# A hybrid decoder block on one core: one copy out of a product's bank queued later, one block's gate values in another buffer, and the first chunk of terms loaded from ScalarE's queue

## The chip, the cores and the metric

The kernel runs on one core of one Trainium2 chip. The metric is the device time of one execution in microseconds (us), as the median of several runs. The core has five engines that each run their own queue of instructions in order and wait for each other through semaphores: TensorE (PE in the profile; it multiplies matrices, its weight loads are listed apart as PEld), VectorE (DVE), ScalarE (ACT), GpSimd (POOL) and SyncE (SP), which here only issues transfers. Transfers (DMA) are issued by SyncE, ScalarE or GpSimd and carried out by 16 DMA engines. TensorE writes its results into banks of PSUM; everything else lies in SBUF.

## The reference

The input is 512 tokens of width 2048 in float32. One RMS norm feeds one input projection, whose columns go to two attention mixers (a dilated sliding window one with 8 heads and a sparse one with compressed, selected and window branches, 8 heads). Their normed outputs go through one output projection and are added to the input. Then comes the part that matters here, a gated feed-forward layer with 5632 hidden columns, and a final norm:

```
hn2 = rmsnorm(h, norm2_g[l])
h = h + (jax.nn.silu(hn2 @ w_gate[l]) * (hn2 @ w_up[l])) @ w_down[l]
return rmsnorm(h, final_g)
```

## The kernel before

**Precision.** A float32 matrix product is made of three products of a faster type. Each operand is split into a high part (a rounded copy, made by ScalarE, L176) and a low part (operand minus high part, made by VectorE, L179), and high by high, high by low and low by high are added in PSUM (L1018 to L1020). A block of weights is 128 x 1024 and arrives by a transfer into a buffer named raw; its two parts go into a buffer named w, of which there are three, so the split for a product can start when the product three places before it has ended.

**Seven products.** The feed-forward layer is computed in blocks of 128 hidden columns, 44 of them (f = 0 to 43). The weights of one block form a 2 x 2 scheme, gate and up by the two halves of the model width; the activations form another, the halves of the width by the two halves of the tokens (LO and HI, 256 tokens each). A scheme of Strassen's kind replaces the eight products of such a 2 x 2 multiplication by seven, P1 to P7, of 24 matmuls each. They run in the order P1, P5, P6, P2, P7, P3, P4 (block 0 in another one). The right operands are seven fixed "terms" of the activations, B11, T1, T2, B21, T3, B22, T4 in that same order, each in a high and a low part; T2, T3 and B22 lie in the tiles named ah and al. The left operands are combinations of the four weight quadrants A11, A12, A21, A22. Y is A21 + A22, made by a load from SyncE and a second load that GpSimd issues and that adds on top (L138); X is A21, or A21 + A11 made in the same way. VectorE makes the further combinations in place (L807).

**Banks.** P1, P6, P7 and P4 accumulate into one bank of PSUM, E; P5 and P3 into F; P2 has G. Between them the bank's value so far has to be taken out: after P1 by g1 (ScalarE, L1128, into the left half of the gate tile g), after P5 by g5 (ScalarE, L1132, into the right half of the tile u), after P6 by g6 (L1135). So P6 may not start before g1 has read E, and P3 not before g5 has read F. VectorE adds the later banks on top, the Silu is taken (L1147), and u becomes the hidden block. g and u are taken from a ring of two buffers with the tag "ft". In block 0 the same is done by gate0: a Silu on ScalarE (L1186) and a multiplication on VectorE (L1187) end it, and these two run while block 1 has begun. A second ring of two buffers, tag "r", serves for factors that are spread over the partitions.

**Down projection.** Pairs of hidden blocks are turned into the seven terms of the next multiplication and stored to DRAM by ScalarE's queue (L1070), in five chunks of eight blocks; the last four hidden blocks stay in SBUF. After block 43 the down projection runs through the chunks, four units per chunk, each unit again seven products in the same order. After each product VectorE adds or subtracts its bank to the residual (down, L1048 and L1051), again before the next product may accumulate into that bank. A chunk's terms are loaded back (fetch, L1077, 512 KB each, a high and a low one per term) into the tiles that the products read. For the first chunk this happens during block 43: when a product has ended, its term is free and the first chunk's data are loaded into it, on SyncE's queue, the high part in the half of a product that follows and the low part one half later.

**What sets the order.** The program is written out by hand. A product counts as two halves, and tick() is called ahead of each half. In every tick come, in this order: the work put down for this half in soon and then in turns (splits and combinations of the next products: the high part four halves ahead of its product, the low part three), then load_to (new loads, as far as buffers are free; six raw buffers in this part), then the work put off with later(n, ...), n halves on. Since each engine runs its instructions in this order, an instruction that waits holds up all that stands behind it on its engine. The split for P2 stands behind g1, the split for P7 behind g5, the split for P3 behind g6.

Transfers issued by SyncE and ScalarE take eight completion semaphores in turn, in the order of the program; the one that takes a semaphore waits until the transfer that had it before has landed.

The functions that the diff touches are these:

Of the kernel before, what the change touches and what calls it, by code (L numbers as in the profile page):

```python
# [11 lines left out]
F32 = mybir.dt.float32  # L12
# [4 lines left out]
S = 512  # L17
# [58 lines left out]
def block_kernel(ctx: ExitStack, tc: tile.TileContext, xt, wst, wdn, smalls, wg, w2c, bias, ident_in, out):  # L76
# [3 lines left out]
    pe, act, dve, pool_e, sp = nc.tensor, nc.scalar, nc.vector, nc.gpsimd, nc.sync  # L80

    base = ctx.enter_context(tc.tile_pool(name="base", bufs=1))
# [108 lines left out]
    k = 2 * units.index(("out", 0, 1))  # L191
# [15 lines left out]
    soon = {}  # L207
# [6 lines left out]
    pos = {"half": 0}  # L214
# [20 lines left out]
    def later(n, f):  # L235
        i = len(lag)
        while i and lag[i - 1][0] > pos["half"] + n:
            i -= 1
        lag.insert(i, (pos["half"] + n, f))
# [65 lines left out]
    def tokens(*accs):  # L305
        return [[a[:, 128 * t:128 * t + 128] for a in accs] for t in range(accs[0].shape[-1] // 128)]
# [46 lines left out]
    for k in range(KB):  # L353
        x = xc.pop(k)
# [137 lines left out]
    def evac(p, tag, scale=None, keep=False):  # L492

        t = tmp()
        if scale is None:
            dve.tensor_tensor(t, p, r1, op=OP.mult)
        else:
            dve.scalar_tensor_tensor(t, p, scale, r1, op0=OP.mult, op1=OP.mult)
        ph, pl = (MH, ML) if tag[0] == "k" else (WH, WL)
        h = placed(kvq(tag), S, ph, tag=tag + "h", name=tag + "h")  # L500
        l = placed(kvq(tag), S, pl, tag=tag + "l", name=tag + "l")
        act.activation(h, t, AF.Copy)
        dve.tensor_tensor(l, t, h.bitcast(F32), op=OP.subtract)
        return (h, l, t) if keep else (h, l)
# [136 lines left out]
    queue = deque()  # L641
# [75 lines left out]
    def proj_block(upto=None):  # L717
        return ps.tile([128, 512], F32, tag="proj", name="pp", bufs=2)
# [40 lines left out]
    for j in range(NH):  # L759
        if j == 4:  # L760
            kv_group(1, False)
        g = j // 4
        bb = load_bias(8 + j)
        ba = load_bias(j)
        p = proj_block()
# [8 lines left out]
        p = proj_block()  # L774
# [3 lines left out]
        p = proj_block()  # L778
        for half in range(2):
            in_unit(p, half)  # L780
        k = evac(p, "ka")
        v = V()
        queue.append(Att("dil", q, k, v, ba, None, {}, True, True, head_done(j, 0)))
        p = proj_block()
# [59 lines left out]
    def out_unit(half, tag="proj"):  # L844
        p = ps.tile([128, 512], F32, tag=tag, name="pab", bufs=2)
        c = 8 - 8 * half
        run_unit([(p, ah[:, c + k, :], al[:, c + k, :], k == 0, k == 7) for k in range(8)])
        return p
# [54 lines left out]
    term = {}  # L903
# [5 lines left out]
    for nb in range(2, KB):  # L909
        while "hs" not in rest and (nb == 4 and not idle() or nb == 2 and (queue or cur["s"])):  # L910
            step()
        p = out_unit(1, ("proj", "sc", "t")[nb // 2 % 3])
# [8 lines left out]
    def ft(name="ft"):  # L921
        return ffn.tile([128, S], F32, tag="ft", name=name, bufs=2)
# [77 lines left out]
    for i in range(KB):  # L1000
        nb = PASS2[i]
        p = out_unit(0)
# [7 lines left out]
    OPERAND = {"P1": "B11", "P2": "B21", "P3": "B22", "P4": "T4", "P5": "T1", "P6": "T2", "P7": "T3"}  # L1010
# [4 lines left out]
    st = {}  # L1015
# [6 lines left out]
    def product(kind, f, m, name):  # L1022

        if kind == "g" and not f:
            key, tag = BANK0[name]
        else:
            key = BANK[name]
            tag = TAG[key]
            if kind == "g" and f == 1:
                tag = {"E": "t", "G": "proj"}.get(key, tag)  # L1030
        new = name in ("P1", "P5", "P2") or (key == name)
        if new and not (name == "P2" and key == "a"):
            st[key] = ps.tile([128, 512], F32, tag=tag, name=key, bufs=1 if tag == "o" else 2)
        else:
            new = False
        p = st[key]
        th, tl = term[OPERAND[name]]
        for k in range(2):
            i = tick()
            job = wide[i - k]  # L1040
            for s in range(4):
                c = slice(512 * k + 128 * s, 512 * k + 128 * s + 128)
                n = 4 * k + s if kind == "g" else 4 * ((f + 1) % 2) + s
                o = p[:, 256 * k:256 * k + 256] if kind == "d" else p[:, :256]
                mm(o, job.h[:, c], job.l[:, c], th[:, n, :], tl[:, n, :], new and k == 0 and s == 0, k == 1 and s == 3)

    def add(o, a, b):
        dve.tensor_tensor(o, a, b, op=OP.add)  # L1048
# [5 lines left out]
    scr = [scp.tile([128, 14 * 1024], F32, name=f"scr{c}") for c in range(NCH)]  # L1054
# [16 lines left out]

    NAMES = ("B11", "T1", "B21", "B22", "T2", "T3", "T4")

    def fetch(c, name, x):
        k = 7 * x + NAMES.index(name)
        n = 4 * ((c + 1) % 2)
        sp.dma_start(term[name][x][:, n:n + 4, :].bitcast(F32), scr[c][:, 1024 * k:1024 * k + 1024].rearrange("p (a b) -> p a b", b=256))  # L1077

    def pair_terms(f, u):

# [39 lines left out]
    def gate(f, name):  # L1120
        p = {k: st[k] for k in "EFG" if k in st}

        def x(k):
            return p[k][:, :256]

        def g1():
            st["g"] = ft()
            act.activation(st["g"][:, LO], x("E"), AF.Copy)  # L1128

        def g5():  # L1130
            st["u"] = ft()
            act.activation(st["u"][:, HI], x("F"), AF.Copy)  # L1132

        def g6():
            act.activation(st["g"][:, HI], x("E"), AF.Copy)  # L1135

        def g2():
            add(st["g"][:, LO], st["g"][:, LO], x("G"))

        def g7():  # L1140
            add(st["u"][:, HI], st["u"][:, HI], x("E"))

        def g3():
            g = st["g"]
            add(g[:, HI], g[:, HI], x("F"))
            dve.tensor_tensor(g, g, st["r2"], op=OP.mult)
            act.activation(g, g, AF.Silu)  # L1147
            later(0, lambda: dve.tensor_tensor(st["u"][:, HI], st["u"][:, HI], g[:, HI], op=OP.mult))

        def g4():  # L1150
            dve.tensor_tensor(st["u"][:, LO], x("E"), st["g"][:, LO], op=OP.mult)

        if name in ("P1", "P5", "P6") and (f, name) != (1, "P5"):
            soon.setdefault(pos["half"], []).append({"P1": g1, "P5": g5, "P6": g6}[name])
        else:
            later(0, {"P5": g5, "P2": g2, "P7": g7, "P3": g3, "P4": g4}[name])
        if name == "P4":
            later(0, lambda: after_gate(f))

    def after_gate(f):  # L1160
        (pair_terms if f < FC else hidden)(f, st["u"])
# [30 lines left out]
    def down(m, name):  # L1192
        p = {k: st[k].rearrange("p (a b) -> p a b", b=256) for k in "EFG" if k in st}
        n1, n2 = slice(2 * m, 2 * m + 2), slice(8 + 2 * m, 10 + 2 * m)
        n, c, op = {"P1": (n1, LO, sub), "P5": (n2, HI, add), "P6": (n1, HI, sub), "P2": (n1, LO, sub),
                    "P7": (n2, HI, add), "P3": (n1, HI, sub), "P4": (n2, LO, add)}[name]
        h = hs[:, n, c]
        later(0, lambda: op(h, h, p[BANK[name]]))

    def scale_in(nb):  # L1200
        dve.tensor_tensor(hs[:, nb, :], hs[:, nb, :], st["inv"], op=OP.mult)

    for kind, f, m in sched:
        order = ORDER if kind == "d" or f else ORDER0
        for i, name in enumerate(order):
            product(kind, f, m, name)
            if kind == "d":
                down(m, name)
                k = 7 * m + i
                if f + 1 < NCH:  # L1210
                    if f:
                        due = [k // 2] if k % 2 else []
                    else:
                        due = [n for n in range(14) if k == 7 + n * 3 // 2]
                    for n in due:
                        later(1, lambda c=f + 1, n=n: fetch(c, OPERAND[ORDER[n // 2]], n % 2))
            elif f:
                gate(f, name)
                if f <= KB and name == "P2":
                    later(1, lambda nb=f - 1: scale_in(nb))  # L1220
                if f == FB - 1:
                    for x in range(2):
                        later(x, lambda name=name, x=x: fetch(0, OPERAND[name], x))
            else:
                if name == "P7":
                    r = st["rs2"] = Rsqrt(tokens(sacc), D, rab.v[:, :4])
                    r.invert()
                    dve.tensor_tensor(r.z, r.z, rab.y[:, :4], op=OP.mult)
                    later(1, lambda r=r: st.update(inv=Spread(r.z, True), r2=Spread(r.y)))
                if name == "P6":  # L1230
                    st["inv"] = st["inv"](False)
                    act.activation(st["rs2"].rs[:, 7, :1], ones[:, :1], AF.Silu)
                    st["r2"] = st["r2"](tag="t", bufs=2)
                    st["u"] = ft()
                gate0(name)
# [153 lines left out]
```

## Time and profile before

| | |
|---|---|
| time, median of 3 runs | 2150.63 us (2144.65 to 2154.28) |
| the profiled execution's own time | 2155.11 us |
| its span, first to last instruction | 2153.3 us |
| mean granted TensorE clock | 0.996 |
| TensorE busy | 2134.8 us, 99% |
| VectorE, ScalarE busy | 1567.5 us (73%), 1012.2 us (47%) |
| DMA | 392.60 MB, mean 182 GB/s |
| block 1 of the feed-forward layer, down projection's first unit | from about 860 us, from about 1705 us |

How to read the rows. A row of the timeline has start, duration, engine, line, operation, the tiles written and read with their shapes, and in brackets how long the engine stood idle before it and what ended that. A row of the waits has who waited, for whom, and then total, number and longest. A row of the windows has the stretch, its length, the busy time (and instructions) of PE, PEld, DVE, ACT and POOL, then the granted clock, the share of the DMA engines and GB/s. A row of the chain of waits has start, duration, engine and tile; for a DMA the duration runs from issue to landing. "DMA to landing" has the shortest, the median and the longest time of the transfers that the question covered.

### The profile page before, as it was taken

The page shows a single profiled execution, that of the slowest core. Times are in us where ns is not written, and L with a number is a line of the kernel's source. Part 1 is how long each engine was busy: PE and PEld are TensorE (multiplying, and loading weights), DVE is VectorE, ACT ScalarE, POOL GpSimd, SP SyncE. Part 2 cuts the span into 40 slices and gives each one's busy share as a digit, 9 for nine tenths or more (in the row PEclk, how much of TensorE's full clock was granted, in tenths as well). Part 3 has the DMA queues.
Part 4 walks back from the last instruction along what each step waited for, and adds up shares of the span by engine and source line. Part 5 has one row for each costly group of instructions (what it writes and reads, how often), then busy time and mean ns, then how long its engine had stood idle before and what let it go on. Part 6 is the DMA issues. An engine that isn't in the chain of part 4 may idle for free.

```text
span 2153.3 us, 37787 instructions
## 1 busy us (share of the span) xinstructions
PE 2134.8 (99%) x15296; PEld 1996.0 (93%) x15296; DVE 1567.5 (73%) x2531; ACT 1012.2 (47%) x1702; POOL 128.9 (6%) x151
## 2 busy tenths in 40 slices
PE   9999999999999999999999999999999999999997
PEld 7888888888888889999999999999999999999997
DVE  6755656366657678888888777877877777888775
ACT  6544444244445255555555455545554433333346
POOL 0000000000000000000000000000000000000003
PEclk9999999999999999999999999999999999999999
DMA  6442222322124334678778877787787799999962
GB/s 226 150 136 81 82 81 69 100 83 87 58 90 143 127 99 127 182 220 239 216 202 235 224 209 234 221 240 209 215 237 221 263 301 292 291 292 284 261 186 79
DMA packets 140511, 392.60 MB, mean 182 GB/s; under 512 B 11952, under 2 KB 50480, under 8 KB 140336
## 3 DMA queue, kind: packets, MB, share of 16 engines
q1 hardware_dynamic: 88592, 298.36, 41.6%
q0 software_dynamic: 15120, 55.06, 14.7%
q10 hardware_dynamic: 36624, 36.77, 4.8%
q8 instruction: 120, 1.97, 0.4%
q14 instruction: 55, 0.45, 0.1%
HBM read 349.24 MB, written 40.89 MB: 181 GB/s over the span
## 4 chain that ended last, share of the span: by engine, by line
PE 92%; DVE 4%; ACT 2%; issue 1%; DMA 1%; ACTq 0%; DVEq 0%; POOLq 0%; SPq 0%
PE E L1020 10%; PE E L1018 10%; PE E L1019 10%; PE pp L210 7%; PE pp L212 7%; PE pp L211 7%; PE F L1020 5%; PE F L1019 5%; PE F L1018 5%; PE pab L210 3%; PE pab L211 3%; PE pab L212 3%; PE G L1020 2%; PE G L1019 2%; PE G L1018 2%
## 5 line engine op out<-in xcount | busy, mean ns | idle before, releaser
L176 ACT ACTIVATE w<-raw 128x1024 fp32r<-128x1024 f32 (+1 forms) x720 | 632.8, 893 | 642.2 <-DVE raw L807 277.9
L179 DVE TENSOR_TENSOR w<-raw,w 128x1024 fp32r<-128x1024 f32 (+1 forms) x720 | 727.8, 1020 | 223.6 <-ACT w L176 221.2
L1018 PE MATMUL E<-ah,w 128*128 128x256 f32 x1008 | 281.1, 279 | 4.0 <-issue 2.2
L1020 PE MATMUL E<-ah,w 128*128 128x256 f32 x1008 | 281.4, 279 | 0.0
L1019 PE MATMUL E<-al,w 128*128 128x256 f32 x1008 | 281.1, 279 | 0.0
L210 PE MATMUL pp<-ah,w 128*128 128x512 f32 x640 | 260.5, 407 | 0.0
L212 PE MATMUL pp<-ah,w 128*128 128x512 f32 x640 | 251.0, 392 | 0.0
L211 PE MATMUL pp<-al,w 128*128 128x512 f32 x640 | 250.2, 391 | 0.0
L1018 PEld LDWEIGHTS E<-ah,w 128*128 128x128 f32 x1008 | 190.3, 189 | 4.4 <-issue 2.3
L1020 PEld LDWEIGHTS E<-ah,w 128*128 128x128 f32 x1008 | 190.6, 189 | 0.0
L1019 PEld LDWEIGHTS E<-al,w 128*128 128x128 f32 x1008 | 190.5, 189 | 0.0
L807 DVE TENSOR_TENSOR raw<-raw 128x1024 f32<-128x1024 f32 x151 | 184.6, 1222 | 2.2
L138 POOL DMA_DIRECT2D raw<-in_wst_dram x105 | 91.1, 868 | 1303.9 <-DMA raw<-in_wst_dram 498.2
L212 PEld LDWEIGHTS pp<-ah,w 128*128 128x128 f32 x640 | 120.2, 188 | 28.3 <-DVE w L179 0.4
L1020 PE MATMUL F<-ah,w 128*128 128x256 f32 x504 | 140.6, 279 | 0.4
L1020 PE MATMUL E<-B11h,w 128*128 128x256 f32 x504 | 140.8, 279 | 0.0
L1019 PE MATMUL E<-B11l,w 128*128 128x256 f32 x504 | 140.7, 279 | 0.0
L1018 PE MATMUL E<-B11h,w 128*128 128x256 f32 x504 | 140.6, 279 | 0.0
L1020 PE MATMUL E<-T4h,w 128*128 128x256 f32 x504 | 140.2, 278 | 0.0
L1019 PE MATMUL E<-T4l,w 128*128 128x256 f32 x504 | 140.1, 278 | 0.0
L1019 PE MATMUL F<-al,w 128*128 128x256 f32 x504 | 140.1, 278 | 0.0
L1018 PE MATMUL E<-T4h,w 128*128 128x256 f32 x504 | 140.1, 278 | 0.0
(341 smaller groups left out, 5214.1 us busy)
## 6 DMA issues: line engine op xcount, KB each, us to landing
raw<-in_wst_dram SPq DMA_DIRECT2D x454, 512.0 KB, 4.8
raw<-in_wst_dram POOLq DMA_DIRECT2D x105, 512.0 KB, 7.3
scr<-ah ACTq DMA_DIRECT2D x20, 896.0 KB, 10.4
scr<-al ACTq DMA_DIRECT2D x20, 896.0 KB, 12.7
ah<-scr SPq DMA_DIRECT2D x15, 512.0 KB, 7.8
al<-scr SPq DMA_DIRECT2D x15, 512.0 KB, 9.5
bias<-in_bias_dram SPq DMA_DIRECT2D x16, 320.0 KB, 3.0
xc<-in_xt_dram SPq DMA_DIRECT2D x16, 256.0 KB, 3.6
```

What stands on the lines that cost most here:

```text
L138: pool_e.dma_start(t, more, accum_op=OP.add)
L176: act.activation(self.h, self.src(), AF.Copy)
L179: dve.tensor_tensor(self.l, self.src(), self.h.bitcast(F32), op=OP.subtract)
L210: pe.matmul(o, wh, mh, start=start, stop=False)
L211: pe.matmul(o, wh, ml, start=False, stop=False)
L212: pe.matmul(o, wl, mh, start=False, stop=stop)
L807: dve.tensor_tensor(raws[u, to], raws[u, to], raws[u, k], op=OP.add)
L1018: pe.matmul(o, wh, mh, start=start, stop=False, skip_group_check=True)
L1019: pe.matmul(o, wh, ml, start=False, stop=False, skip_group_check=True)
L1020: pe.matmul(o, wl, mh, start=False, stop=stop, skip_group_check=True)
```

## The change

Three edits.

1. The copy of P5's bank (g5) is put into soon three halves after the point where it stood. It then comes ahead of the second half of P2, behind the split for P3 on ScalarE, instead of ahead of the split for P7. In block 1, where it stood among the work put off with later, it is now treated like the others.
2. In block 1 the gate tile g comes from the ring "r" and not from "ft". After that, g and u have changed places in the ring "ft".
3. The first chunk's terms are fetched on ScalarE's queue. Both parts of a term are queued in the half that follows the product, ahead of the splits of that half, behind the copy if there is one.

```
-    def fetch(c, name, x):
+    def fetch(c, name, x, queue=sp):
         k = 7 * x + NAMES.index(name)
         n = 4 * ((c + 1) % 2)
-        sp.dma_start(term[name][x][:, n:n + 4, :].bitcast(F32), scr[c][:, 1024 * k:1024 * k + 1024].rearrange("p (a b) -> p a b", b=256))
+        queue.dma_start(term[name][x][:, n:n + 4, :].bitcast(F32), scr[c][:, 1024 * k:1024 * k + 1024].rearrange("p (a b) -> p a b", b=256))
...
         def g1():
-            st["g"] = ft()
+            st["g"] = ft() if f > 1 else base.tile([128, S], F32, tag="r", name="r", bufs=2)
             act.activation(st["g"][:, LO], x("E"), AF.Copy)
...
-        if name in ("P1", "P5", "P6") and (f, name) != (1, "P5"):
-            soon.setdefault(pos["half"], []).append({"P1": g1, "P5": g5, "P6": g6}[name])
+        if name in ("P1", "P5", "P6"):
+            soon.setdefault(pos["half"] + (3 if name == "P5" else 0), []).append({"P1": g1, "P5": g5, "P6": g6}[name])
         else:
-            later(0, {"P5": g5, "P2": g2, "P7": g7, "P3": g3, "P4": g4}[name])
+            later(0, {"P2": g2, "P7": g7, "P3": g3, "P4": g4}[name])
...
                 if f == FB - 1:
                     for x in range(2):
-                        later(x, lambda name=name, x=x: fetch(0, OPERAND[name], x))
+                        soon.setdefault(pos["half"], []).append(lambda name=name, x=x: fetch(0, OPERAND[name], x, act))
```

## The prediction

> **What bounds the kernel now.** Read first was the page's top, then what TensorE waited for, then the clock in three stretches.
>
> ```profile
> span 2153.3 us, 37787 instructions
> ...
> PE 2134.8 (99%) x15296; PEld 1996.0 (93%) x15296; DVE 1567.5 (73%) x2531; ACT 1012.2 (47%) x1702; POOL 128.9 (6%) x151
> ```
> ```profile
> PE E L1018 <- issue: 2.2, 1, 2.2
> PE E L1018 <- ACT ft L1128: 1.9, 1, 1.9
> ...
> ACT ft L1132 <- DVE al L1061: 78.4, 39, 2.6
> ```
> ```profile
> 867.90:871.30 3.40, 3.40 (x18) 3.40 (x18) 2.70 (x3) 0.91 (x3) 0.00 (x0) 0.52 0.01 2
> 1714.50:1717.90 3.40, 3.40 (x18) 3.40 (x18) 2.79 (x4) 1.06 (x1) 0.00 (x0) 0.50 1.06 386
> 656.00:660.00 4.00, 3.14 (x18) 2.59 (x17) 3.37 (x10) 3.27 (x8) 0.00 (x0) 1.00 0.02 3
> ```
> TensorE is busy for all but 18.5 us (2153.3 - 2134.8), so only its stalls can be won. In the feed-forward part there are two, once each: 1.9 us until L1128, and 2.2 us with no releaser named. Behind each, a stretch of 3.4 us ran at a clock of about 0.5; an idle of 0.86 us (4.00 - 3.14) at 657 lowered nothing. The 78.4 us in front of L1132, the copy of P5's bank, are waits of ScalarE, and no wait of TensorE names that line.
>
> I call the stalls A (865 us, block 1) and B (1711 us, P6 of the first down unit, "unit 44"). Their prices:
>
> ```profile
> 865.26 0.28 PE L1020 MATMUL F<-T1h,w 128*128 128x256 f32 x1
> ...
> 867.39 0.38 PE L1018 MATMUL E<-ah,w 128*128 128x256 f32 x1 [1.86 <-ACT ft L1128]
> ...
> 871.85 0.28 PE L1018 MATMUL G<-B21h,w 128*128 128x256 f32 x1
> ...
> 874.68 0.28 PE L1018 MATMUL E<-ah,w 128*128 128x256 f32 x1
> ...
> 877.51 0.28 PE L1018 MATMUL F<-ah,w 128*128 128x256 f32 x1
> ...
> 1710.72 0.28 PE L1020 MATMUL F<-T1h,w 128*128 128x256 f32 x1
> ...
> 1713.18 0.36 PE L1018 MATMUL E<-ah,w 128*128 128x256 f32 x1 [2.18 <-issue]
> ```
> An undisturbed product takes 24 matmuls, 871.85 to 874.68, so 0.118 us each. A: from P5's last matmul (865.26) to P2's first (871.85) are 25 steps, 2.95 us, and 6.59 passed: **3.64 us lost**, some 2.0 of it waiting and 1.6 at the low clock. B: 2.46 passed instead of 0.12, then 3.4 us at half clock, 1.7: **4.04 us lost**. If both went entirely, 7.7 us would be won, 0.36%.
>
> **Part 1: another buffer for block 1's gate values (stall A).**
>
> ```profile
> 865.16 0.63 ACT L1186 ACTIVATE ft<-ft 128x512 f32<-128x512 f32 x1 [2.20 <-DVE ft L1185]
> 866.96 0.38 ACT L1128 ACTIVATE ft<-E 128x256 f32<-128x256 f32 x1 [1.17 <-DVE ft L1187]
> ...
> 871.05 0.63 ACT L1057 ACTIVATE ah<-ft 128x512 fp32r<-128x512 f32 x1 [2.49 <-DVE ft L1051]
> 871.59 1.04 ACT L176 ACTIVATE w<-raw 128x1024 fp32r<-128x1024 f32 x1
> ```
> ```profile
> 876.16 1.23 DVE L179 TENSOR_TENSOR w<-raw,w 128x1024 fp32r<-128x1024 f32 x1 [1.13 <-ACT w L176]
> ```
> L1128 copies P1's bank E, into which P6 accumulates next; it waited for L1187 because its buffer was block 0's gate buffer. The new buffer, of tag "r", last held the factors that were spread for the residual before block 1 began, so it is free. What is late next is the Silu in front of the copy on ScalarE's queue: it starts at 865.16, and behind an activation of that width the next starts 0.54 us later (871.05 to 871.59). So the copy starts at 865.70, 1.26 us earlier, and P6 at about 866.13; 0.75 us of the waiting stay, less than the 0.86 us that lowered no clock. TensorE would then be 2.9 us ahead (3.64 - 0.75), but the splits behind the copy, which ScalarE and VectorE hand to each other, move by 1.26 us only. The tightest is P3's: its low half was ready at 877.39 (876.16 + 1.23), wanted by P3's third matmul at 877.75 (877.51 + two steps). In future that is 876.13, and the gain there is 877.75 - 876.13 = **1.6 us**, taken. Bounds: 3.6 (whole stall) and -0.4 (1.26 less a low-clock stretch of 1.7).
>
> **Part 2: P5's copy three half-products later.** Nothing is added; block 1's copy moves with the rest. Queued behind the waiting copy is P7's split, which now starts up to 2.6 us earlier. What hides this is TensorE's own work: no stall of TensorE in blocks 2 to 43. The copy must still precede P3, which accumulates into its bank.
>
> ```profile
> 894.66 1.06 ACT L176 ACTIVATE w<-raw 128x1024 fp32r<-128x1024 f32 x1 [2.16 <-DVE raw L807]
> 894.75 0.39 ACTq L1070 DMA_DIRECT2D scr<-ah  x1
> 895.17 0.59 ACTq L1070 DMA_DIRECT2D scr<-al  x1
> 895.63 1.05 ACT L176 ACTIVATE w<-raw 128x1024 fp32r<-128x1024 f32 x1
> ```
> ```profile
> 896.91 0.28 PE L1018 MATMUL F<-ah,w 128*128 128x256 f32 x1
> ```
> It goes behind P3's split, ready in block 2 at 895.72 (894.66 + 1.06); copied by about 896.1 (0.38 more), 0.8 us before P3's 896.91. **0 us.** Without that cover each microsecond of lateness costs one per block, 42 in all.
>
> **Part 3: fourteen loads of terms from ScalarE's queue (stall B).** Why does P6 wait at 1711?
>
> ```profile
> 1692.13 3.59 DMA raw<-in_wst_dram
> ...
> 1696.40 9.35 DMA raw<-in_wst_dram
> 1705.86 1.07 ACT w L176
> ```
> ```profile
> 1690.85 1.22 DVE L807 TENSOR_TENSOR raw<-raw 128x1024 f32<-128x1024 f32 x1
> ...
> 1712.40 0.68 DVE L1051 TENSOR_TENSOR hs<-hs,E 128x512 f32<-128x512 f32 x1
> ```
> By the chain of waits, unit 44's combined block Y is late. SyncE loads it at 1692.13, as soon as L807 frees a buffer (1690.85 + 1.22), GpSimd adds the second half on top at 1696.40, and it lands at 1705.75. From there splits and combinations run without a pause of TensorE's making to L1051 (1712.40 to 1713.08), which reads bank E before P6 may write it. So P6 starts 7.4 us after Y lands, and every microsecond of Y's lateness is one of P6's. Three things touch Y.
>
> First, the issues. The pair behind P1 (B11) goes in front of P2's split on ScalarE.
>
> ```profile
> 1688.34 0.39 ACT L1128 ACTIVATE ft<-E 128x256 f32<-128x256 f32 x1 [0.44 <-PE E L1020]
> 1688.62 1.05 ACT L176 ACTIVATE w<-raw 128x1024 fp32r<-128x1024 f32 x1
> ...
> 1699.64 1.06 ACT L176 ACTIVATE w<-raw 128x1024 fp32r<-128x1024 f32 x1 [1.76 <-PE E L1020]
> ```
> A pair issued by ScalarE takes 0.97 us from activation to activation (894.66 to 895.63); here only the 0.28 us to 1688.62 cover it, so the split, P2's low half, L807 and Y's load move by **0.7 us** (0 to 1.0). The other six pairs cost the same where ScalarE idles anyway (1.76 us at 1699.64).
>
> Second, the rings. Before, all loads sat in SyncE's ring.
>
> ```profile
> 1695.62 0.81 SPq L136 DMA_DIRECT2D raw<-in_wst_dram  x2
> ...
> 1701.23 0.32 SPq L1077 DMA_DIRECT2D B21l<-scr  x1
> ...
> 1704.62 0.32 SPq L1077 DMA_DIRECT2D ah<-scr  x1
> ```
> ```profile
> DMA to landing us min/median/max: 5.6/7.1/8.5
> ...
> DMA to landing us min/median/max: 5.3/5.3/5.3
> ```
> ```profile
> 1704.00:1716.00 12.00, 9.82 (x77) 9.48 (x76) 8.42 (x10) 4.64 (x6) 0.89 (x1) 0.94 1.02 406
> ```
> The engines are full here (1.02 at 406 GB/s, so a load of 512 KB takes 1.3 us of them). With T1's pair issued at P5's end (a product of 2.8 us after 1688.3, so 1691.1) and T2's at 1693.9 in another ring, Y's load shares where it was alone: I take **1.0 us** more (0 to 1.3, one load between). Then the accumulate: alone it landed after 5.3 us (that of 1671.57), beside one full ring after 9.35. A second full ring slips in once more as much as the accumulate itself moves, 512 KB: **1.3 us** (0 to 4.0, the price of the first ring).
>
> The Trainium skill (DMA: Bandwidth & Descriptors, Issuing engines are not separate DMA queues, and Queues, rings and completion order) speaks against this part: the issuing engines share the same 16 DMA engines, which take turns between rings packet by packet, so another queue saves issue time only. By it, the 1.0 and 1.3 belong in the sum; without sharing Part 3 would cost 0.7 alone.
>
> Third, a wait that is added. The transfers of SyncE and ScalarE take eight completion counters in turn, and none is issued before the eighth before it has landed: B21l at 1701.23, just as the block load of 1695.62 (+5.6) was in, T3's at 1704.62 after that of 1696.04 (+8.5). SyncE bore this. Now T3's pair holds ScalarE until those same two block loads land, about 1704.6, and behind it stands P1's split of unit 44 (1699.64 before). Its low half is then ready 1.06 + 1.23 later, 1706.9; P1 is due at 1705.2 (two products before P6's 1710.8), its third matmul at 1705.4, so P1 waits 1.5 us. Nothing is added by that, because P6 still hangs on Y. On SyncE nothing is won: Y's load waits for its buffer, not for a fetch.
>
> Sum of Part 3: Y lands 0.7 + 1.0 + 1.3 = 3.0 us later, P6 starts at 1716.2. TensorE loses that in waits before P1, P5 and P6; a low-clock stretch after P6 costs 1.7 as before. **+3.0 us**, bounds -4.0 (stall gone) and +8.0 (1.0 + 1.3 + 4.0 and one more low-clock stretch).
>
> On the clock the Trainium skill (TensorE: Matmul & The Clock Gate, Part 1) has it that the gate closes after a window of some 3.4 us without work. By that B's waits would lower nothing and the sum be 1.7 less; the rows at 867.90 and 1714.50 show waits of 1.9 and 2.2 us doing it, and I keep the charge.
>
> **The sum:** -1.6 + 0 + 3.0 = **+1.4 us**. The profiled execution took 2155.11 us (span 2153.3), 4.5 above the median of the three timed runs, 2150.63; it becomes 2156.5, the median **2152.0**.
>
> **The rivals.**
> Both stalls go. For it: the fetches start earlier, T3's by 5 us (P7's end, 1699.6, against 1704.62), and block loads no longer stand behind fetches in SyncE's queue. Against: Y's load stood behind none. If the accumulate lands by 1703.4 (1710.8 - 7.4), B's 4.0 vanish with 1.6 to 3.6 of A: -5.6 to -7.6, about 2144.
> Y later still. If a second full ring costs what the first did, 4.0, and one more stretch runs slow: 0.7 + 1.0 + 4.0 + 1.7 - 1.6 = +5.8, 2156.4. For it: 9.35 against 5.3; against: the two rings need not be full all that time.
> The moved copy holds up P3, slower than before: place, bank F in each of blocks 2 to 43; it decides once P3's split is ready 0.8 us later than in the block shown; at 0.3 us beyond that, 42 x 0.3 = +12.6, 2163. Against it: P7's split moves earlier, not later.
> The change doesn't do what it says: the copy in block 1 waits as long as before, for the Silu. Then A gives 0 and the sum is +3.0, 2153.6; the Silu's row starts 1.8 us before the copy's (865.16 against 866.96), so I fold this into the forecast.
>
> **How the numbers follow.** Forecast 0.48 (own range 2148 to 2155), both stalls gone 0.28, Y later still 0.19, the copy 0.05. The range takes the two middle rivals and the spread of the three runs (2144.65 to 2154.28): 2142 to 2159. What this measurement can tell from no change is about 0.5%, 10.8 us; only the copy's case passes it, and run spread may lift the first two rivals over it, so faster 0.05, same 0.89, slower 0.06.
>
> **What would show it.** Right: a wait of about 0.7 us before P6 in block 1 with no slow stretch behind it, and short ones before P7 or P3; L1132 idles no more on L1061; unit 44's accumulate lands more than 10 us after issue, ScalarE idle before its first split, P6 still waiting. Wrong: clock 1.0 throughout unit 44, or any wait of TensorE on L1132.

## The result and the profile after

The changed kernel takes 2136.82 us (2135.31 to 2137.10, five runs) against 2150.63 (2144.65 to 2154.28, five runs with those shown above): a ratio of 0.9936, interval 0.9918 to 0.9953. That is 13.8 us faster and 5 us below the lower end of the range, where 1.4 us slower was forecast. The profiled execution took 2136.06 us, its span 2134.3. The profiled execution of before took 2155.11 us, 4.5 above its median, so the two traces lie 19.0 us apart and the medians 13.8.

The page's top after:

```profile
span 2134.3 us, 37797 instructions
...
PE 2112.6 (99%) x15296; PEld 1973.8 (92%) x15296; DVE 1569.9 (74%) x2531; ACT 1015.9 (48%) x1702; POOL 128.9 (6%) x151
```

TensorE's busy time itself fell, from 2134.8 to 2112.6 us, with the same 15296 matmuls. The waits outside of it grew: 21.7 us (2134.3 - 2112.6) against 18.5. So the time was not won in stalls. The stretches of the feed-forward part tell where; the windows of before and then of after are, row by row, blocks 2 to 42, blocks 43 and 44 (44 is the first down unit), units 45 to 48, and units 49 to 62. The columns are the stretch, its length, and the busy time of PE, PEld, DVE, ACT and POOL with their instructions, then the clock.

```profile
883.16:1685.26 802.10, 801.74 (x6891) 801.13 (x6889) 643.37 (x811) 410.62 (x570) 52.88 (x61) 1.00 0.78 222
1685.26:1728.92 43.66, 41.48 (x338) 41.14 (x337) 31.05 (x36) 17.23 (x20) 2.62 (x3) 0.96 0.88 313
1728.92:1808.12 79.20, 79.20 (x674) 79.20 (x673) 62.25 (x66) 29.73 (x28) 6.93 (x8) 1.00 0.98 288
1808.12:2075.31 267.19, 267.19 (x2354) 267.19 (x2353) 215.05 (x225) 104.19 (x98) 24.25 (x28) 1.00 0.95 274
```
```profile
882.10:1664.49 782.39, 782.39 (x6890) 782.39 (x6889) 645.80 (x812) 414.58 (x570) 52.88 (x61) 1.00 0.79 227
1664.49:1712.48 47.99, 41.76 (x338) 40.59 (x337) 32.00 (x37) 17.16 (x20) 2.63 (x3) 0.96 0.86 287
1712.48:1788.79 76.31, 76.31 (x674) 76.31 (x673) 61.38 (x65) 29.78 (x28) 6.93 (x8) 1.00 0.98 296
1788.79:2055.99 267.20, 267.20 (x2354) 267.20 (x2353) 215.09 (x225) 104.20 (x98) 24.25 (x28) 1.00 0.96 275
```

The first rows hold the answer. In both kernels TensorE works without a pause (0.36 us of idle in 802.10 before, none after) at a clock of 1.00, and the same 41 blocks, 6888 matmuls of equal shape, take **19.71 us less**. One step from a matmul to the next has become shorter. Blocks 43 and 44 lose 4.33 us, units 45 to 48 win 2.89, block 1 wins 1.47 (23.49 to 22.02), and some 0.7 is lost at the two ends: together the 19.0 us between the spans.

Read block by block (168 matmuls), the starts of the matmuls have two widths. A **narrow** step is 113.3 ns, a block of them 19.04 us (19.20 in blocks 2, 5, 9 ... 41, where P1's weights lie at another offset in the buffer, the code's argument "even", and P1's steps are 120 ns). A **wide** step is 117.8 ns, a block 19.79 us. After, all blocks from 2 to 42 are narrow. Before, narrow steps begin behind such an "even" P1 (behind 8 of 11; in blocks 17, 29 and 41 the steps stay wide) and end in a P3, eight times in blocks 2 to 43. The timeline of before at such an end, block 6, and what is upstream of it:

```profile
969.28 0.39 ACT L1132 ACTIVATE ft<-F 128x256 f32<-128x256 f32 x1 [1.71 <-DVE al L1061]
969.56 1.05 ACT L176 ACTIVATE w<-raw 128x1024 fp32r<-128x1024 f32 x1
...
971.79 1.22 DVE L807 TENSOR_TENSOR raw<-raw 128x1024 f32<-128x1024 f32 x1
...
973.04 1.06 ACT L176 ACTIVATE w<-raw 128x1024 fp32r<-128x1024 f32 x1 [2.15 <-DVE raw L807]
...
974.14 1.23 DVE L179 TENSOR_TENSOR w<-raw,w 128x1024 fp32r<-128x1024 f32 x1 [1.13 <-ACT w L176]
...
974.93 0.28 PE L1018 MATMUL F<-ah,w 128*128 128x256 f32 x1
975.04 0.28 PE L1019 MATMUL F<-al,w 128*128 128x256 f32 x1
...
975.42 0.39 PE L1020 MATMUL F<-ah,w 128*128 128x256 f32 x1
```

P5's copy (L1132) waits until 969.28, P7's split stands behind it, then comes the combination for P3 (L807), P3's high half at 973.04 and its low half at 974.14. That ends at 975.37. P3's third matmul, the first that needs the low half, would have started at 975.16 (one step behind 975.04) and starts at 975.42. From here on every step is wide. The view of the matmuls' waits has no row for this. The view of the weight loads' waits has one: in the trace the weights of a matmul are loaded one step ahead of it (the load for the one at 975.04 starts at 974.93), and in blocks 2 to 42 of before three such loads waited for a low half, 1.0 us in all, in blocks 6, 10 and 14:

```profile
PEld F L1020 <- DVE w L179: 1.0, 3, 0.3
```

The same block after:

```profile
964.36 1.05 ACT L176 ACTIVATE w<-raw 128x1024 fp32r<-128x1024 f32 x1
...
967.12 1.22 DVE L807 TENSOR_TENSOR raw<-raw 128x1024 f32<-128x1024 f32 x1
...
968.43 1.06 ACT L176 ACTIVATE w<-raw 128x1024 fp32r<-128x1024 f32 x1 [1.11 <-DVE raw L807]
969.40 0.36 ACT L1132 ACTIVATE ft<-F 128x256 f32<-128x256 f32 x1
969.53 1.23 DVE L179 TENSOR_TENSOR w<-raw,w 128x1024 fp32r<-128x1024 f32 x1 [1.19 <-ACT w L176]
```
```profile
972.17 0.28 PE L1018 MATMUL F<-ah,w 128*128 128x256 f32 x1
972.29 0.28 PE L1019 MATMUL F<-al,w 128*128 128x256 f32 x1
972.40 0.28 PE L1020 MATMUL F<-ah,w 128*128 128x256 f32 x1
```

P7's split no longer stands behind the copy and starts 7.8 us ahead of P3 (972.17 - 964.36), not 5.4 (974.93 - 969.56). The low half is ready at 970.76, 1.64 us before it is wanted, and the steps stay at 0.11.

### The profile page after: what moved, and what is told of

Same layout as the page of the kernel before. It is cut to its first block, busy times and chain, and to the rows that moved or that the text cites. A ratio compares the mean times of both kernels' runs of the same rounds, so it can differ in the third digit from the quotient of the medians.

```text
span 2134.3 us, 37797 instructions
## 1 busy us (share of the span) xinstructions
PE 2112.6 (99%) x15296; PEld 1973.8 (92%) x15296; DVE 1569.9 (74%) x2531; ACT 1015.9 (48%) x1702; POOL 128.9 (6%) x151
## 3 DMA queue, kind: packets, MB, share of 16 engines
q8 instruction: 120, 1.97, 0.4%
## 4 chain that ended last, share of the span: by engine, by line
PE 96%; DVE 2%; ACT 1%; DMA 0%; issue 0%; ACTq 0%; DVEq 0%
PE E L1018 11%; PE E L1019 11%; PE E L1020 10%; PE pp L210 7%; PE pp L212 7%; PE pp L211 7%; PE F L1020 5%; PE F L1018 5%; PE F L1019 5%; PE pab L210 3%; PE pab L211 3%; PE pab L212 3%; PE G L1019 3%; PE G L1020 3%; PE G L1018 3%; PE pt L580 1%
## 5 line engine op out<-in xcount | busy, mean ns | idle before, releaser
L179 DVE TENSOR_TENSOR w<-raw,w 128x1024 fp32r<-128x1024 f32 (+1 forms) x720 | 727.8, 1020 | 195.5 <-ACT w L176 193.7
L1018 PE MATMUL E<-ah,w 128*128 128x256 f32 x1008 | 279.1, 277 | 1.8 <-issue 1.2
L1020 PE MATMUL E<-ah,w 128*128 128x256 f32 x1008 | 278.8, 277 | 0.2 <-DVE w L179 0.2
L1018 PEld LDWEIGHTS E<-ah,w 128*128 128x128 f32 x1008 | 189.3, 188 | 2.5 <-issue 1.6
L1020 PEld LDWEIGHTS E<-ah,w 128*128 128x128 f32 x1008 | 189.3, 188 | 0.4 <-DVE w L179 0.4
L807 DVE TENSOR_TENSOR raw<-raw 128x1024 f32<-128x1024 f32 x151 | 184.5, 1222 | 2.2
L1018 PE MATMUL F<-T1h,w 128*128 128x256 f32 x504 | 140.1, 278 | 2.5 <-ACT w L176 2.5
L1018 PE MATMUL E<-B11h,w 128*128 128x256 f32 x504 | 140.4, 279 | 1.0 <-ACT w L176 1.0
L1020 PE MATMUL E<-B11h,w 128*128 128x256 f32 x504 | 140.4, 279 | 0.8 <-DVE w L179 0.8
L1020 PE MATMUL F<-T1h,w 128*128 128x256 f32 x504 | 140.2, 278 | 0.8 <-DVE w L179 0.8
L1019 PE MATMUL F<-T1l,w 128*128 128x256 f32 x504 | 139.9, 278 | 0.0
L1020 PE MATMUL F<-ah,w 128*128 128x256 f32 x504 | 139.5, 277 | 0.4 <-DVE w L179 0.4
L1020 PE MATMUL E<-T4h,w 128*128 128x256 f32 x504 | 139.4, 277 | 0.0
```

Source lines behind the costliest of these rows:

```text
L179: dve.tensor_tensor(self.l, self.src(), self.h.bitcast(F32), op=OP.subtract)
L807: dve.tensor_tensor(raws[u, to], raws[u, to], raws[u, k], op=OP.add)
L1018: pe.matmul(o, wh, mh, start=start, stop=False, skip_group_check=True)
L1019: pe.matmul(o, wh, ml, start=False, stop=False, skip_group_check=True)
L1020: pe.matmul(o, wl, mh, start=False, stop=stop, skip_group_check=True)
```

## The experiments

The theory tested: the step's width is a state. It becomes wide where P3's low half comes late or at the last moment, and stays so until something makes it narrow, as an "even" P1 does. Rivals: that the stalls or the transfers gave the time; that VectorE's or ScalarE's work beside TensorE sets the step; that a late half costs its own wait alone.

All kernels in one table. Stretches are from each one's profiled execution; the last column counts the changes from narrow to wide steps in blocks 2 to 43, all of which begin in P3.

| kernel | median us (lowest to highest) | ratio to before, interval | block 1 | blocks 2-42 | 43-44 | 45-48 | to wide |
|---|---|---|---|---|---|---|---|
| before | 2150.63 | | 23.49 | 802.10 | 43.66 | 79.20 | 8 |
| after | 2136.82 | 0.9936, 0.9918-0.9953 | 22.02 | 782.39 | 47.99 | 76.31 | 0 |
| e1 copy alone | 2134.82 (2133.24-2137.59) | 0.9924, 0.9908-0.9941 | 23.49 | 782.39 | 43.87 | 79.20 | 0 |
| e2 buffer alone | 2149.99 (2147.97-2153.37) | 1.0000, 0.9990-1.0009 | 22.02 | 797.96 | 44.19 | 76.32 | 7 |
| e3 fetch alone | 2154.19 (2150.23-2158.30) | 1.0018, 1.0008-1.0028 | 23.09 | 802.31 | 46.46 | 76.31 | 9 |
| e4 copy and buffer | 2133.23 (2131.10-2135.42) | 0.9918, 0.9903-0.9932 | 21.82 | 782.40 | 43.68 | 76.32 | 0 |
| e6 after, no "even" P1 | 2147.60 (2131.33-2178.89) | 0.9958, 0.9939-0.9977 (the eight lower of ten runs) | 21.82 | 780.64 | 46.87 | 79.14 | 0 |
| e7 before, "even" in every 2nd block | 2148.41 (2147.08-2149.07) | 0.9970, 0.9959-0.9980 | 23.29 | 797.42 | 44.28 | 76.47 | 11 |
| e8a late half behind "even" P1 | 2166.01 (2163.96-2171.93) | 1.0058, 1.0036-1.0080 | 21.82 | 812.84 | 43.16 | 79.20 | 7 |
| e8b late half ahead of it | 2147.17 (2145.08-2152.54) | 0.9967, 0.9957-0.9977 | 21.82 | 800.28 | 42.82 | 79.85 | 8 |
| e5 copy, buffer, Y first | 2131.63 (2131.06-2133.76) | 0.9899, 0.9884-0.9913 | 21.82 | 782.40 | 39.34 | 80.28 | 0 |
| e5b after, Y first | 2132.18 (2131.20-2133.89) | 0.9901, 0.9885-0.9918 | 21.82 | 782.39 | 43.39 | 76.31 | 0 |
| e9 as e5, few "even" P1s | 2126.72 (2125.95-2128.28) | 0.9875, 0.9860-0.9890 | 21.82 | 781.85 | 39.57 | 78.08 | 1 |

Three groups were run on three chips, each with its own runs of before: e1 to e4 (before 2150.51), e6 to e8b (2154.0), and e5, e5b, e9 (2153.64).

**The three parts alone (e1, e2, e3) and the first two (e4).** The diffs are the parts of the diff above: its last hunk but one in e1, the line of `st["g"]` in e2, `queue` and `act` in e3.

> The kernel before with the copy of P5's bank queued three half-products later, and nothing else. Theory (step width): the gain of 13.8 us is TensorE's step from matmul to matmul. In a block that runs undisturbed it is 113.3 ns (a block takes 19.04 us), in the others 117.7 ns (19.79 us); before, P3's low half came just as P3's third matmul wanted it, in the even blocks above all, and from there to the next block whose P1 weights lie at the other offset every step was wide. The moved copy lets P7's split, and so P3's, come earlier. So this edit alone brings blocks 2 to 42 to 19.04 us each (19.20 where P1 lies at the other offset), some 782 us for the 41 of them against 802, and a time 11 to 18 us below before; the stalls of block 1 and of the first down unit stay. Rival (stalls): the gain comes from the other two edits, which act on the two stalls; then this kernel takes what before takes, within 3 us, with blocks of 19.79 us.

> The kernel before with block 1's gate values in the other ring, and nothing else. Step width: block 1 goes from 23.5 to about 22.0 us, as in the changed kernel, and nothing else changes: 1 to 2 us below before, the wide blocks still there. Stalls: a good part of the 13.8 us, 5 or more.

> The kernel before with the first chunk's terms fetched on ScalarE's queue, and nothing else. Step width: block 43 and the first down unit together go from 43.7 to about 48 us, as in the changed kernel, because unit 44's combined weights land later and ScalarE waits for earlier transfers to land: about 4 us above before, if the runs' spread lets it be seen. Stalls: 5 us or more below before.

> The moved copy and the other buffer, the fetch on SyncE's queue as before. Step width: faster than the changed kernel by what its fetch cost there (block 43 and the first down unit 47.99 against 43.67 us), so about 4 us below it, near 2132.5 us. Stalls: slower than the changed kernel.

The copy alone gives all of the step's gain, with block 1's stall untouched (15.7 us below its before, 11 to 18 expected):

```profile
883.32:1665.71 782.39, 782.39 (x6891) 782.39 (x6889) 645.63 (x811) 414.56 (x570) 52.87 (x61) 1.00 0.79 227
```

The buffer alone shortens block 1 by 1.47 us and no more can be told in its time. The fetch alone makes the two blocks where it acts 2.80 us longer (43.66 to 46.46, about 48 expected). e4 took 2133.23 us, 2132.5 expected. In before, e2, e3 and e7, the four kernels whose copy is early, P3 began a wide stretch 35 times in blocks 2 to 43; in after, e1, e4, e5, e5b and e6, whose copy is late, never, and in e9, also late, once. That the transfers or the stalls gave the time is out.

How near the low half has to come can be read from the traces of these eleven kernels. In blocks 2 to 43, TensorE came to P3 with narrow steps 382 times. The table sorts these by when the low half ended, against the moment at which the third matmul was due (one step behind the second):

| low half ended | cases | steps wide from there |
|---|---|---|
| 0.04 to 0.27 us late | 16 | 16 |
| 0.05 to 0.07 us early | 5 | 5 |
| 0.16 us early | 27 | 15 |
| 0.20 us early or more | 334 | 0 |

So a low half need not be late for the steps to become wide: of the eight times in before, three are in the first row, one in the second and four in the third. The late copy puts every block of after into the last row, at 0.6 us or more.

**No "even" P1 (e6).** What makes the steps narrow?

```
-        for job in quad_jobs(n_units + 4 * i, ORDER if i else ORDER0, i == 2 or i % 4 == 1, i in OWN):
+        for job in quad_jobs(n_units + 4 * i, ORDER if i else ORDER0, False, i in OWN):
```

> The changed kernel, but the weights of P1 never lie at the other offset (the first products of block 2 and of every fourth block did). Step-width theory: TensorE's steps of 113.3 ns begin only at such a P1, so every block from 2 on takes 19.79 us instead of 19.04; 41 blocks of 0.75 us and some 19 down units of 0.73 us are about 44 us, so about 2181 us. Rival (the time was won by fewer waits for the copy or the splits, the offset has nothing to do with it): 16 first products of 0.16 us less, 2134 us.

The theory's "only at such a P1" fell; its size, 0.75 us a block, holds in the trace. Of ten runs one took 2131.33, seven 2146.75 to 2149.11, two 2178.13 and 2178.89. The profiled run is one of the seven. A wait before P3 in block 1, and then the windows of blocks 2 to 42 and 49 to 62:

```profile
876.05 0.38 PE L1020 MATMUL F<-ah,w 128*128 128x256 f32 x1 [0.39 <-DVE w L179]
```
```profile
881.37:1662.01 780.64, 780.64 (x6890) 780.64 (x6889) 645.83 (x812) 414.57 (x570) 52.99 (x61) 1.00 0.78 228
...
1788.02:2065.04 277.02, 277.02 (x2355) 277.02 (x2354) 215.51 (x225) 104.06 (x98) 24.32 (x28) 1.00 0.92 265
```

Here the steps became narrow behind that wait of 0.39 us, stayed so for 41 blocks of 19.04 us, became wide in unit 44's waits, and stayed so to the end: 277.02 us where after needs 267.20. So a wait can leave either width behind. From the lowest run to the seven are some 16 us, of which units 45 to 62 would explain 12.7 (79.14 + 277.02 against 76.31 + 267.20). The lowest run and the two highest have no trace, so this is argued, and nothing is built on the two highest.

**"Even" P1 in every second block of before (e7).** The condition becomes `i == 2 or i % 2 == 1`.

> The kernel before, with P1's weights at the other offset in every second block instead of every fourth. Step-width theory: a stretch of wide steps that a late low half began ends after at most two blocks instead of four, so of the 20 us that the wide stretches of blocks 2 to 42 cost, at least a third goes, less 10 first products of 0.16 us: 2140 to 2146 us. Rival (the time hangs on waits, not on the step): 1.6 us more, 2152 us.

Too much was expected. 5.6 us were won (2154.0 to 2148.41), 4.7 of them in blocks 2 to 42. The trace has 11 returns to wide steps there, each in a P3: two in a block whose own P1 was "even", the other nine in the block behind one. Narrow steps bring TensorE to P3 earlier, and a split that keeps its pace is then late or nearly so: in before, the low half comes 0.77 us ahead of the third matmul in most wide blocks, and 0.33 us ahead at most in narrow ones. Nor does an "even" P1 always end the wide steps: in blocks 2 to 43 of all the traces it met them 66 times and left them wide 15 times, six of these in e7.

**A late half on purpose (e8a, e8b).** On the kernel of e4, VectorE repeats the low half of P3 (`last[-2]`) in ten blocks.

```
+            for _ in range(self.times):
+                dve.tensor_tensor(self.l, self.src(), self.h.bitcast(F32), op=OP.subtract)
...
+            job.times = 3 if kind == "g" and 4 <= i < 42 and i % 4 == 1 and job is last[-2] else 1
```

e8b has `i % 4 == 0`.

> Parts 1 and 2 of the change, and P3's low half is computed three times over in blocks 5, 9 ... 41 (VectorE repeats the same subtraction), so that it comes about 1 us after P3 wants it; P1 of the same block has just had its weights at the other offset. Step-width theory: each of these 10 blocks waits about 1 us, and the 22 products that follow until the next such P1 run with wide steps, 0.106 us each: 10 x (1.0 + 2.3) = 33 us more than parts 1 and 2 alone, about 2166 us. Rival (a late half costs its own wait and nothing after): 10 us more, 2143 us, and no more than with the late half in blocks 4, 8 ... 40.

> As the run with the late low half in blocks 5 to 41, but in blocks 4, 8 ... 40: the same 10 repeats and the same waits, one product ahead of a P1 whose weights lie at the other offset. Step-width theory: only P4 runs with wide steps, so 10 x (1.0 + 0.1) = 11 us more than parts 1 and 2 alone, about 2144 us, and some 22 us less than its twin. Rival (own wait only, or VectorE's added work): the same time as its twin.

The twins differ by 18.8 us (22 expected). Not all of that is steps. The late matmul starts 1.46 us behind the one before it in most of e8a's ten blocks, and in most of e8b's 1.03, together 5.7 us; and in the two traces blocks 2 to 42 lie 12.6 us apart (812.84 against 800.28), since e8b's profiled execution, 2152.54 us, is its slowest. In e8a (L181 there is L179 of the others, L1022 to L1024 are L1018 to L1020), first the late half of block 9, then the windows of block 9 and the block behind it, and of blocks 21 and 22:

```profile
1030.22 0.28 PE L1023 MATMUL F<-al,w 128*128 128x256 f32 x1
1031.69 0.38 PE L1024 MATMUL F<-ah,w 128*128 128x256 f32 x1 [1.19 <-DVE w L181]
```
```profile
1016.35:1037.21 20.86, 19.67 (x171) 19.48 (x169) 17.84 (x21) 9.95 (x14) 1.74 (x2) 1.00 0.75 199
1037.21:1056.99 19.78, 19.78 (x170) 19.78 (x169) 16.79 (x24) 10.38 (x14) 0.86 (x1) 1.00 0.83 251
...
1256.98:1277.63 20.65, 19.47 (x171) 19.27 (x169) 17.50 (x21) 9.95 (x14) 1.73 (x2) 1.00 0.68 175
1277.63:1296.67 19.04, 19.04 (x171) 19.04 (x169) 15.93 (x22) 10.31 (x14) 0.86 (x1) 1.00 0.82 247
```

Block 10 has no repeat and no wait, and takes 19.78 us; block 22 behind an equal wait takes 19.04. Seven of the ten late halves turned the steps wide. Six times they stayed wide until the next "even" P1, and from block 41 until the one after it. Three late halves (blocks 5, 21, 37) did not turn them. So a late half costs more than its own wait, and what it leaves behind outlasts it: that is shown. VectorE's added work as the cause is out, since it is not there in block 10. That it happens each time, as the theory had it, is not so. In e8b the steps stayed wide behind the "even" P1s of blocks 9, 13 and 41 and of unit 45. e8a took 2166.01 us where about 2166 was expected, e8b 2147.17 where about 2144 was.

**Y first (e5, e5b).** Block Y of unit 44 is loaded ahead of A11 (and X ahead of A12), without and with the fetch on ScalarE.

```
-        names = ("A11", "Y", "A12", "X", "A22") if own or u == n_units else ...
+        names = ("A11", "Y", "A12", "X", "A22") if own and u != n_units + 4 * FB or u == n_units else ...
```

> Parts 1 and 2 of the change without part 3, and unit 44's combined block Y is loaded ahead of its plain block A11, the order that block 43 has not. If Y's late landing is what P6 of unit 44 waits for, the two waits there (0.75 and 2.17 us) and the low clock behind them go: 4 to 5 us below parts 1 and 2 alone (2133.2), 2128 to 2129 us. Rival (P1 then waits for A11 as long as P6 waited for Y): no change.

> The whole change, and unit 44's Y loaded ahead of A11. If part 3 costs what it does by making Y late, it costs nothing here: within 1 us of the kernel that has parts 1 and 2 and Y first. If it costs what it does because ScalarE stands behind its own loads of terms, P1 and P5 of unit 44 still wait and it is 2 to 4 us slower than that kernel.

In blocks 43 and 44 both theories' first halves hold: 39.34 us against e4's 43.68, so stall B's 4.3 us are Y's; and with the fetch on ScalarE 43.39, so 4.05 us of Part 3 remain with Y early. But the medians lie 0.55 us apart (2131.63 and 2132.18; 2128 to 2129 was expected of e5). The windows of blocks 43 and 44 and of units 45 to 48, of e5 and then of e5b:

```profile
1664.47:1703.81 39.34, 38.92 (x339) 38.54 (x337) 29.21 (x34) 16.89 (x20) 1.72 (x2) 1.00 0.93 329
1703.81:1784.09 80.28, 79.59 (x674) 79.21 (x673) 63.85 (x68) 29.85 (x29) 7.83 (x9) 1.00 0.98 293
```
```profile
1664.19:1707.58 43.39, 39.85 (x338) 39.09 (x337) 31.99 (x37) 17.13 (x20) 2.56 (x3) 1.00 0.93 320
1707.58:1783.89 76.31, 76.31 (x674) 76.31 (x673) 61.39 (x65) 29.80 (x28) 6.95 (x8) 1.00 0.96 295
```

What e5 wins in the first stretch it gives back in the second, where its steps are wide and e5b's narrow. Which of the two comes out of unit 45 is as open as in e6.

**Few "even" P1s (e9).** On e5's kernel only the first products of blocks 1, 2, 45 and 46 keep the other offset (`i in (1, 2, 45, 46)`).

> As parts 1 and 2 with Y first, but only the first products of blocks 1, 2, 45 and 46 have their weights at the other offset. If narrow steps, once begun, last until a weight half or a copy comes late, then the other 15 such products were only a price of 0.16 us each: 2.4 us less, 2126 us, with no block of 19.79 us from 2 to 43. If they decay by themselves, blocks after 6 turn wide, and it takes up to 40 us more.

2126.72 us, 26.9 below before on the same chip and the fastest here. That is 4.9 us below e5, of which 2.4 were expected from the "even" P1s and 2.2 lie in units 45 to 48. The steps stayed narrow for 39 blocks (2 to 40), with no "even" P1 behind block 2. They then became wide in block 41's P3, so "no block of 19.79 us from 2 to 43" fell. Its low half ended at 1638.41 (1637.18 + 1.23) for a third matmul at 1638.46: again a half that came at the last moment. No decay without such a cause is seen.

## Why the prediction was wrong

**Its first reading failed: "TensorE is busy for all but 18.5 us, so only its stalls can be won."** Busy time is not a constant of the work: the same matmuls took 22.2 us less of it. The prediction measured one product (871.85 to 874.68, 0.118 us a matmul) and called it undisturbed; that stretch lay in block 1 and was wide. Block 22 of before, with the same 168 matmuls at the same clock, would have shown 19.04 us where block 3 takes 19.79:

```profile
1275.72:1294.76 19.04, 19.04 (x171) 19.04 (x169) 15.71 (x22) 10.31 (x14) 0.86 (x1) 1.00 0.80 211
```

**The step that failed is Part 2's "0 us".** Its premises were right: nothing added, P7's split starts up to 2.6 us earlier, the copy in front of P3 in time. What was wrong is the cover: "TensorE's own work: no stall of TensorE in blocks 2 to 43". The prediction followed P3's high half and the copy to P3's first matmul at 896.91, and stopped there. P3's low half in the same block of before, and the two matmuls behind the quoted one:

```profile
895.75 1.23 DVE L179 TENSOR_TENSOR w<-raw,w 128x1024 fp32r<-128x1024 f32 x1 [1.13 <-ACT w L176]
...
897.03 0.28 PE L1019 MATMUL F<-al,w 128*128 128x256 f32 x1
897.14 0.28 PE L1020 MATMUL F<-ah,w 128*128 128x256 f32 x1
```

It ended at 896.98, 0.16 us before the third matmul. In this very product the steps of before turned from narrow to wide for the first time. Part 1 had traced that same half in block 1 ("the tightest is P3's"); Part 2 did not carry it over to 41 blocks. In place of 0, Part 2 brought 19.71 us in blocks 2 to 42 of the profiled executions (e1: the same), 15.7 between the medians of e1 and its before. What moved it is that P7's split, and P3's behind it, no longer stand behind the copy, so that P3's low half comes in time for narrow steps. The rival that the moved copy holds up P3 had the right place, bank F's P3 in each block, and the opposite sign.

**Part 1 was right.** 1.6 us were taken, block 1 shows 1.47. The copy starts behind the Silu as worked out, and the first wait is 0.59, not 0.75. Timeline of after, ScalarE and then TensorE, and the window behind the wait:

```profile
865.58 0.63 ACT L1186 ACTIVATE ft<-ft 128x512 f32<-128x512 f32 x1 [2.21 <-DVE ft L1185]
866.12 0.36 ACT L1128 ACTIVATE r<-E 128x256 f32<-128x256 f32 x1
```
```profile
866.54 0.38 PE L1018 MATMUL E<-ah,w 128*128 128x256 f32 x1 [0.59 <-ACT r L1128]
...
873.09 0.39 PE L1020 MATMUL E<-ah,w 128*128 128x256 f32 x1 [0.19 <-DVE w L179]
...
876.58 0.39 PE L1020 MATMUL F<-ah,w 128*128 128x256 f32 x1 [0.40 <-DVE w L179]
```
```profile
867.00:870.40 3.40, 3.40 (x31) 3.40 (x30) 2.98 (x4) 0.91 (x3) 0.00 (x0) 1.00 0.00 0
```

The clock behind it stayed at 1.00, and the splits for P7 and P3 ate the rest in waits of 0.19 and 0.40, as the prediction said. Its reason for the clock, a wait shorter than one that lowered nothing, is not safe: in e1 two idles of 0.75 and 0.76 us came just before 3.4 us at a clock of 0.50.

**Part 3 had the sign and the mechanism, and its terms were mis-sized.** +3.0 was taken, +4.33 measured in blocks 43 and 44 (after against e4: +4.31), and +2.80 for the fetch alone (e3). After's chain of waits at Y, ScalarE behind its own loads, TensorE's waits in unit 44 and the window behind the longest:

```profile
1680.06 10.06 DMA raw<-in_wst_dram
```
```profile
1683.61 1.06 ACT L176 ACTIVATE w<-raw 128x1024 fp32r<-128x1024 f32 x1 [5.13 <-DMA al<-scr]
```
```profile
1684.72 0.39 PE L1018 MATMUL E<-B11h,w 128*128 128x256 f32 x1 [1.02 <-ACT w L176]
1685.98 0.39 PE L1020 MATMUL E<-B11h,w 128*128 128x256 f32 x1 [0.76 <-DVE w L179]
...
1691.31 0.38 PE L1018 MATMUL F<-T1h,w 128*128 128x256 f32 x1 [2.47 <-ACT w L176]
```
```profile
1692.60:1696.00 3.40, 3.40 (x17) 3.40 (x18) 2.89 (x4) 2.13 (x3) 0.89 (x1) 0.55 1.03 422
```

Y's load goes out 0.6 us later after its block began than in e4 (0.7 taken). Beside ScalarE's ring the plain load lands 7.5 us after its issue, 3.6 in e4, so 3.9 us later, 1.0 taken. The accumulate itself takes 10.06 us against 9.51 in e4, so 0.6, 1.3 taken. Y thus lands some 5 us later, not 3.0, and P6 starts 5.0 us later than in e4 (32.98 against 27.94 us behind block 43's start). In e3 the same three terms are 0.8, 2.3 and 0.6 against before. P1's wait, 1.5 us forecast, came as 1.02 and 0.76. ScalarE did stand still ahead of P1's split, as forecast, but for the landing of T2's low part, which it had queued itself, and not for a block load.

The forecast took Part 3 for Y's lateness alone. In e5b it costs 4.05 us although Y has long landed (its accumulate is issued at 1664.13 and lands 5.2 us later). Waits of 0.27 and 0.75 us before P1 follow from ScalarE standing behind its loads, and by e5b's chain of waits so does the wait of 1.97 us before P6:

```profile
1675.53 9.31 DMA raw<-in_wst_dram
1684.87 0.33 ACTq L1077
1685.29 1.07 ACT w L176
```

A load of a term (L1077) is issued only when a block load has landed, and P5's split stands behind it; the combination and the split for P6 follow. So "nothing is added by that, because P6 still hangs on Y" holds only while Y is late.

**All the signs of being right came true and the time did not.** The short wait at full clock, the waits before P7 and P3, no idle of L1132 on L1061 in blocks 2 to 43, an accumulate of more than 10 us, ScalarE idle and P6 waiting 0.68 us are all in the trace of after. They test the waits that the prediction looked at; none of them looks at the step between matmuls.

**The spread.** The prediction scaled its sum from a profiled execution 4.5 us above the median and widened the range by the spread of the runs, 9.6 us. After, five runs lie within 1.8. That fits a kernel whose wide stretches fall differently in each execution, but other runs of before have no trace, so it is argued.

## What to carry to other kernels

Before taking TensorE's busy time as given, measure the step between matmuls in several stretches: equal work at equal clock that takes 4% longer in one than in another is time to be won, and the views of waits list little or none of it. Ask for the waits of the weight loads too: here they held the one row that named P3's low half. Follow both halves of each operand to the first matmul that reads them, in every block of the loop, and treat slack of less than about 0.2 us as lateness, as the table of margins has it for this kernel. When a short stall is removed or added, look at the steps behind it before booking the gain.

## What was not expected of the hardware

- The step between 256-column matmuls, each with its own weight load, is 113.3 or 117.8 ns at a granted clock of 1.00, and 120 ns in products whose weights lie at the other offset. Either width lasts for hundreds of matmuls (41 blocks in e6). The Trainium skill (TensorE: Matmul & The Clock Gate, Back-to-back issue gap) gives N/2.4 + 2.5 ns for an isolated matmul, by which an estimate for 256 columns is 109.2 ns, and says that in a stream of weight loads and matmuls both set the spacing. The trace has two widths for one and the same stream, and it decides.
- A matmul that had to wait for its weights left narrow steps behind in some cases and wide ones in others: wide in all 16 cases of a half late by 0.04 to 0.27 us and in all eight of e8b that met narrow steps (0.9 to 1.0 us late), wide seven times and narrow three times in e8a (some 1.3 us late), narrow behind the wait of 0.39 us in e6's block 1. What decides between them, and why the other offset mostly ends in narrow steps, stays open.
- An idle of 2.47 us was followed by 3.4 us at a clock of 0.55, but one of 2.0 us in e5b's unit 44 by none, its two blocks at 1.00; 1.86 us had lowered it before, and so, in e1, did two idles of 0.75 and 0.76 us, 1.3 us apart. The length of one idle alone does not decide in this range.
